# Where SBUF operands start modulo 512 bytes, and a third buffer for the stick-breaking weights, in a hybrid attention layer

## The chip, the core and the metric

The kernel runs on one core of a Trainium2 chip. A core has the matrix engine TensorE (PE; its weight loads are shown apart as PEld), VectorE (DVE), ScalarE (ACT), GpSimd (POOL) and SyncE (SP), which here only issues DMAs. The engines share the memory SBUF, 128 partitions wide; PE writes its results to PSUM, which has eight banks of 512 fp32 columns. Each engine takes its instructions in the order of its own program, and engines wait for each other by semaphores. The metric is the device time of one execution in microseconds (us), the median over the runs.

## The reference

One decoder layer on 1024 tokens of 1024 channels. The parts that matter here:

```python
u = rms_norm(h, norm1_g) * (1 + scale1) + shift1
z = u @ w_in                    # queries, keys, values, gates of both attentions, m_a, m_b
y_a = nsa_attention(...) @ w_up_nsa            # 8 heads of 64, sparse attention
y_b = stick_breaking_attention(q_b, k_b, v_b) @ w_up_sb      # 8 heads of 64
h = h + gate1 * ((sigmoid(m_a) * y_a + sigmoid(m_b) * y_b) @ w_out)
u2 = rms_norm(h, norm2_g) * (1 + scale2) + shift2
h = h + gate2 * (square(relu(u2 @ mlp_w1)) @ mlp_w2)         # 4096 hidden channels

def stick_breaking_attention(q, k, v):         # per block of 128 queries
    z = einsum('bqhd,bshd->bhqs', q, k) * 64 ** -0.5
    mask = key_pos < query_pos
    log_keep = where(mask, log_sigmoid(-z), 0)
    suffix = cumsum(log_keep, reverse) - log_keep
    a = where(mask, exp(log_sigmoid(z) + suffix), 0)
    return a @ v
```

So a weight is sigmoid(z) times the product of sigmoid(-z) over the keys between it and the query. All is in float32.

## The kernel before

Every large product is done in three: each operand is split into a high part, rounded to the matmul's fp32r type, and a low part, the rest (`hi` and `lo`, L63 and L66 among others), and PE adds high by high, high by low and low by high. A matmul has a stationary operand of 128 columns, loaded first, and a moving operand, mostly of 512 columns; a matmul below is named by its line. In its rows "px<-mth,wh" the first name behind the arrow is the moving operand, the second the stationary one.

The stages follow each other on PE, in us of the profiled span: loading and the first projections (0 to 120), keys and values of the sparse attention (L588, to 186), the sparse attention (214 to 604), the stick-breaking attention (623 to 857), the up projections of both attentions' outputs (L1324, 879 to 973), the output projection (L1428, to 1084) and the MLP (to the end). The rest of the input projection (L746) is cut into units and laid between the matmuls of the two attentions as filling; 96 of its matmuls run alone from 857 to 879.

In the up projection a unit is 12 matmuls of L1324 into one PSUM bank: four blocks of 128 channels, three products each, with the weights' parts wh and wl stationary and the attention output's parts oh and ol moving. Units of the two attentions (branch 0, sparse; branch 1, stick-breaking) alternate; oh and ol of the two branches lie in two pools, and wh and wl in one. In the MLP a hidden unit is 24 matmuls of L1512 with weights wh, wl stationary and the normalised input mth, mtl moving, 64 units in all. The second product of the MLP (L1561) is done by seven products of half-size blocks instead of eight, with the hidden activations' parts rah, ral stationary and the second weights' parts wbh, wbl moving.

Stick-breaking goes head by head, with three kinds of chunks: kind 0 is query rows 0 to 3 (of 128 queries each) with all their keys, 512, 384, 256 and 128 of them; kind 1 is rows 4 to 7 with their last 512 keys; kind 2 is rows 4 to 7 with their earlier keys, 512 down to 128. A chunk takes these steps:
- PE: scores into one of three PSUM banks psx (L1123 and L1124 with the key's two parts, L1126 adds the diagonal's mask).
- ACT: sigmoid of the scores into a tile sig (L1128), and sigmoid of their negatives in place in the bank (L1129). The tile is named sigr in kind 1 (five buffers), and after its width in kinds 0 and 2 (sig512, sig384, sig256, sig128; two buffers each).
- DVE: a running product over the bank, backwards, into a tile Pt (L1138). After it the bank can take another chunk.
- POOL: sig times Pt, in place (L1140).
- PE: the finished 128x128 pieces of sig are transposed into a bank pt (L1155); ACT and DVE split it into th and tl (L1163, L1164), and PE multiplies these with the values into the bank po (L1175).

The sig tile is free for another chunk when the last transposes out of it are done.

The kernel's code gives the work in a sequence; a scheduler then orders each engine's instructions, from its own estimates of their durations and from what has to wait for what, the reuse of buffers included. Tiles come from pools, stacked from the left or the right end of SBUF: a pool's offset follows from the sizes of those stacked before it on its side. A tile's place modulo 512 bytes in its partition therefore hangs on all tiles before it.

Of the kernel before, what the change touches and what calls it, by code (L numbers as in the profile page):

```python
# [6 lines left out]
F32 = mybir.dt.float32  # L7
# [10 lines left out]
NT = 8  # L18
# [17 lines left out]
def build(tc, I, out):  # L36
# [3 lines left out]
    def pool(name, side=None, bufs=1, **kw):  # L40
        if side:
            kw.update(side=side, reuse_waits="tile")
        p = tc.alloc_tile_pool(name=name, bufs=bufs, **kw)
        opened.append(p)
        return p
# [80 lines left out]
    pre_l = pre.tile([128, NK, 128], F32R, name="uwl")  # L126
    p1a = pool("p1a", "left")

    pool("odd", "right").tile([128, 8], F32, name="odd")
    xt_pool = pool("xt", "right")  # L130


# [263 lines left out]
    kvp = pool("kv", "right")  # L396
    kT = kvp.tile([128, 4, S], F32R, name="kT")
    vS = kvp.tile([128, NT, 4, 2, HD], F32R, name="vS")
    kcT = kvp.tile([128, 2, HD], F32R, name="kcT")
    gates = kvp.tile([128, NT, 8, 3], F32, name="gates")  # L400
    vC = kvp.tile([HD, 2, 2, HD], F32R, name="vC")
    bnp = pool("bn", "right")
    Bn = bnp.tile([128, 8, 256], F32, name="Bn")
# [177 lines left out]

    def kv_mm(t):
        raw = pb.tile([128, 544], F32, name="kvr", bufs=2)
        for c, (c0, c1) in enumerate(((0, 272), (272, 536))):
            p = (pd, psx)[c]()
            for k in range(NK):
                for n, (a, b) in enumerate(three(k, slice(t * 128, (t + 1) * 128))):
                    nc.tensor.matmul(p[:, :c1 - c0], a, ws[k][b][:, c0:c1],  # L588
                                     start=(k == 0 and n == 0), stop=(k == NK - 1 and n == 2))
            nc.scalar.copy(raw[:, c0:c1], p[:, :c1 - c0])  # L590
        return raw
# [59 lines left out]
    for n, (kind, t) in enumerate(jobs):  # L651
# [8 lines left out]
        if kind == "q":  # L660
            b = q_mm(t)
# [6 lines left out]
        else:  # L668
            if t == 0:
                ws = wk  # L670
            b = kv_mm(t)
# [86 lines left out]
    at = pool("at", "right")  # L758
# [43 lines left out]

    PT_ = 0.216


    def nsa_a(i, kv, hp, qT, P):
        n0, n1 = max(0, i - 1), i + 1
        x0 = 256 - (n1 - n0) * 128
        nb = 8 * i + 8
        chunks = plan(i)  # L810
        ngm = at.tile([128, 2, 2, 3], F32, name="ngm", bufs=2)
        sms = at.tile([128, 2, 2, 3], F32, name="sms", bufs=2)
        if len(chunks) < 6:
            nc.vector.memset(ngm, 3e38)
            nc.vector.memset(sms, 0.0)
# [1 line left out]
        for g in range(2):  # L817
            h = kv * 4 + hp * 2 + g
            q0, q1 = qT[0][:, hp * 2 + g], qT[1][:, hp * 2 + g]
            for br, c, a, b in chunks:  # L820
                n = (b - a) * 128
                p = psx()
# [26 lines left out]
        p = psx()  # L849
        for g in range(2):  # L850
            for q in range(2):
# [3 lines left out]
        sc = at.tile([128, 2, HD], F32, name="sc", bufs=2)  # L855
        nc.vector.tensor_tensor(sc[:, :, :nb], p[:, :128].rearrange("p (g c) -> p g c", g=2)[:, :, :nb],
                                Bc[:, kv * 4 + hp * 2:kv * 4 + hp * 2 + 2, 56 - 8 * i:56 - 8 * i + nb], op=OP.add)
        mc = at.tile([128, 2], F32, name="mc", bufs=2)
        nc.vector.tensor_reduce(mc, sc[:, :, :nb], axis=AX.X, op=OP.max, negate=True)
        nc.vector.scalar_tensor_tensor(sc[:, :, :nb], mc[:, :, None].to_broadcast([128, 2, nb]), 1e20, sc[:, :, :nb],  # L860
                                       op0=OP.min, op1=OP.add)
        pcx = at.tile([128, 2, HD], F32, name="pcx", bufs=2)
        P["c"] = pcx

        mm = at.tile([128, 2, 2], F32, name="mm", bufs=2)
        nc.vector.tensor_reduce(mm, ngm, axis=AX.X, op=OP.min)
        fc = at.tile([128, 2, 2, 3], F32, name="fc", bufs=2)
        nc.vector.tensor_tensor(fc, mm[:, :, :, None].to_broadcast([128, 2, 2, 3]), ngm, op=OP.subtract)
        yield 0.43
        nc.scalar.activation(pcx[:, :, :nb], sc[:, :, :nb], AF.Exp)  # L870
        nc.scalar.activation(fc, fc, AF.Exp)
        yield 0.0
        tot = at.tile([128, 3, 2], F32, name="tot", bufs=2)
        nc.vector.tensor_reduce(tot[:, 0], pcx[:, :, :nb], axis=AX.X, op=OP.add)
        nc.vector.tensor_tensor(sms, sms, fc, op=OP.mult)
        nc.vector.tensor_reduce(tot[:, 1:3], sms, axis=AX.X, op=OP.add)
# [10 lines left out]
    def nsa_b(i, kv, hp, P):  # L887
# [66 lines left out]
            yield cost  # L954
        tmp = at.tile([64, 256], F32, name="otmp", bufs=2)
        nc.scalar.copy(tmp, po_[64:128, :256])
        o = at.tile([64, 256], F32, name="osum", bufs=2)
        nc.vector.tensor_tensor(o, po_[0:64, :256], tmp, op=OP.add)
        h0 = (kv * 4 + hp * 2) * HD
        nc.sync.dma_start(oa_d[h0:h0 + 128, i * 128:(i + 1) * 128].rearrange("(g d) q -> d g q", g=2),  # L960
# [93 lines left out]


    def sb_gens(sp):
        zero = sp.tile([128, 16], F32, name="zero")[:, 0:1]
        nc.vector.memset(zero, 0.0)

        def load(u, h):  # L1060
# [54 lines left out]
        def sb_a(kind, chunk, ops, A, edges):  # L1115

            i, c0, c1 = chunk
            Q, Kh, Kl = ops
            w = c1 - c0
            p = psx()  # L1120
            qs = Q[:, i * 128:(i + 1) * 128]
            diag = kind != 2
            track(nc.tensor.matmul(p[:, :w], qs, Kh[:, c0:c1], start=True, stop=False))  # L1123
            track(nc.tensor.matmul(p[:, :w], qs, Kl[:, c0:c1], start=False, stop=not diag))  # L1124
            if diag:
                track(nc.tensor.matmul(p[:, w - 128:w], identr, diagr, start=False, stop=True))  # L1126
            sig = sp.tile([128, w], F32, name="sigr" if kind == 1 else "sig%d" % w, bufs=5 if kind == 1 else 2)
            nc.scalar.activation(sig, p[:, :w], AF.Sigmoid, scale=HD ** -0.5)  # L1128
            nc.scalar.activation(p[:, :w], p[:, :w], AF.Sigmoid, scale=-(HD ** -0.5))  # L1129
            A[i, kind] = (sig, c0)  # L1130

            def fin():
                Pt = sp.tile([128, 528], F32, name="Pt", bufs=6)
                if diag:
                    nc.vector.memset(Pt[:, w:w + 1], 1.0)
                else:
                    nc.vector.tensor_copy(Pt[:, w:w + 1], edges.pop(i)[:, 0:1])
                nc.vector.tensor_tensor_scan(Pt[:, 0:w][:, ::-1], p[:, 0:w][:, ::-1], zero.to_broadcast([128, w]),  # L1138
                                             1.0 if diag else Pt[:, w:w + 1], op0=OP.mult, op1=OP.add)
                nc.gpsimd.tensor_tensor(sig, sig, Pt[:, 1:w + 1], op=OP.mult)  # L1140
                if kind == 1:
                    edges[i] = Pt
            return fin, max(w, 256) * 2 / 2400.
# [469 lines left out]
```

## Time and profile before

| | us |
|---|---|
| median of three runs | 1754.13 (1746.5 to 1754.78) |
| the profiled execution, whole | 1753.26 |
| its span, first to last instruction | 1751.5 |
| PE busy, share of the span | 1694.7, 97% |
| DVE, POOL, ACT busy | 1141.8, 876.1, 819.8 |
| TensorE's mean granted clock | 0.989 |

The profile's busy times say which engine has work at all times; the table by stage says in which stretch PE has gaps. A matmul's duration in the rows reaches past the start of the next one, because matmuls are pipelined: what one costs in a row of them is the difference between starts. A wait stands in brackets behind the instruction that waited, with what released it.

### The profile page before, as it was taken

The numbers are of one execution on the slowest core, as the hardware profiler recorded it, in microseconds if no ns is written. First come the engines' busy times: TensorE is split into PE (matmuls) and PEld (weight loads), VectorE is DVE, ScalarE is ACT, GpSimd is POOL, SyncE is SP. The second block draws the span as 40 slices with busy tenths as digits, with TensorE's granted clock in tenths as the row PEclk, the third lists the DMA queues.
The fourth block names the chain that finished last, engine by engine and source line by source line (L and its number), as shares of the span: only waits on it lengthen the run. The fifth ranks groups of instructions, "written<-read, shape, count | busy, mean of one in ns | idle before, by whom it ended". The sixth has DMA issues, their size and how long they took to land.

```text
span 1751.5 us, 25194 instructions
## 1 busy us (share of the span) xinstructions
PE 1694.7 (97%) x8652; PEld 1414.9 (81%) x8652; DVE 1141.8 (65%) x2514; ACT 819.8 (47%) x1809; POOL 876.1 (50%) x824
## 2 busy tenths in 40 slices
PE   5999999999999989999999899999999999999998
PEld 4879888888888867788778688888888888888886
DVE  7597478778777567878464564365656575756458
ACT  6433476666666466766433244333333333333332
POOL 0021143434333387865164400786857675858676
PEclk8999999999999989999999999999999999999999
DMA  9365311111121264531485611121212020202102
GB/s 304 97 185 160 109 46 55 55 54 54 49 61 38 62 167 124 157 88 46 135 256 183 216 37 73 38 71 37 70 39 73 25 73 25 72 25 72 41 21 97
DMA packets 153656, 157.14 MB, mean 90 GB/s; under 512 B 13544, under 2 KB 117688, under 8 KB 153528
## 3 DMA queue, kind: packets, MB, share of 16 engines
q1 hardware_dynamic: 149304, 153.42, 29.3%
q10 hardware_dynamic: 4224, 2.10, 0.4%
q8 instruction: 69, 1.13, 0.3%
q14 instruction: 59, 0.48, 0.1%
HBM read 128.21 MB, written 27.28 MB: 89 GB/s over the span
## 4 chain that ended last, share of the span: by engine, by line
PE 83%; DMA 5%; DVE 4%; POOL 3%; ACT 3%; issue 2%; SPq 1%; POOLq 0%; DVEq 0%; ACTq 0%
PE px L1512 20%; PE px L1561 16%; PE pd L746 15%; PE px L1428 5%; PE po L909 4%; PE pt L943 4%; PE px L1324 3%; DMA adraw<-in_ada_w_dram 2%; PE psx L825 2%; PE psx L826 2%; PE cb L302 1%; PE pd L588 1%; PE po L1175 1%; PE psx L588 1%; PE pt L1155 1%
## 5 line engine op out<-in xcount | busy, mean ns | idle before, releaser
L1564 DVE TENSOR_TENSOR acc<-acc,px 128x512 f32<-128x512 f32 x384 | 243.9, 683 | 119.8 <-PE px L1561 114.5
L1512 PE MATMUL px<-mtl,wh 128*128 128x512 f32 x512 | 202.9, 396 | 0.0
L1512 PE MATMUL px<-mth,wl 128*128 128x512 f32 x512 | 202.7, 396 | 0.0
L1512 PE MATMUL px<-mth,wh 128*128 128x512 f32 x512 | 202.5, 396 | 0.0
L746 PE MATMUL pd<-uh,uwh 128*128 128x512 f32 x448 | 181.3, 405 | 0.7 <-ACT zo L1018 0.7
L1561 PE MATMUL px<-wbl,rah 128*128 128x512 f32 x448 | 175.3, 391 | 2.2 <-POOL wbl L1537 1.9
L746 PE MATMUL pd<-ul,uwh 128*128 128x512 f32 x448 | 177.1, 395 | 0.0
L746 PE MATMUL pd<-uh,uwl 128*128 128x512 f32 x448 | 177.1, 395 | 0.0
L1561 PE MATMUL px<-wbh,ral 128*128 128x512 f32 x448 | 174.9, 390 | 0.0
L66 DVE TENSOR_TENSOR wl<-raw,wh 128x1024 fp32r<-128x1024 f32 x48 | 76.3, 1591 | 149.1 <-ACT wh L61 128.7
L1561 PE MATMUL px<-wbh,rah 128*128 128x512 f32 x448 | 172.1, 389 | 0.0
L1537 POOL TENSOR_TENSOR wbl<-raw,wbh 128x1024 fp32r<-128x1024 f32 x40 | 106.0, 2649 | 91.9 <-ACT wbh L1536 91.6
L1523 POOL TENSOR_TENSOR w<-w,grow 128x1024 f32<-128x1024 f32 x32 | 82.8, 2602 | 97.0 <-DVE grow L1296 96.4
L901 DVE TENSOR_TENSOR tl<-pt,th 128x512 fp32r<-128x512 f32 (+8 forms) x168 | 103.7, 620 | 34.3 <-ACT th L900 33.0
L1535 POOL TENSOR_TENSOR raw<-r 128x512 f32<-128x512 f32 x80 | 109.9, 1397 | 20.0 <-DVE wl L66 17.9
L900 ACT CAST th<-pt 128x512 fp32r<-128x512 f32 (+8 forms) x168 | 88.8, 531 | 60.6 <-PE pt L943 58.0
L1512 PEld LDWEIGHTS px<-mth,wl 128*128 128x128 f32 x512 | 96.2, 188 | 23.6 <-issue 0.5
L1512 PEld LDWEIGHTS px<-mtl,wh 128*128 128x128 f32 x512 | 96.3, 188 | 23.0 <-issue 0.2
L1512 PEld LDWEIGHTS px<-mth,wh 128*128 128x128 f32 x512 | 96.2, 188 | 22.9 <-issue 0.2
L1536 ACT CAST rah<-raw 128x1024 fp32r<-128x1024 f32 x40 | 42.1, 1052 | 153.1 <-PE px L1561 139.7
L1561 PEld LDWEIGHTS px<-wbl,rah 128*128 128x128 f32 x448 | 84.1, 188 | 22.1 <-POOL wbl L1537 3.1
L746 PEld LDWEIGHTS pd<-uh,uwl 128*128 128x128 f32 x448 | 84.7, 189 | 18.1
(322 smaller groups left out, 4548.3 us busy)
## 6 DMA issues: line engine op xcount, KB each, us to landing
raw<-in_mlp_w_dram SPq DMA_DIRECT2D x32, 512.0 KB, 4.0
w<-in_mlp_w_dram SPq DMA_DIRECT2D x32, 512.0 KB, 4.0
z_d<-zo SPq DMA_DIRECT2D x56, 256.0 KB, 2.2
uwr<-in_w_in_dram SPq DMA_DIRECT2D x54, 256.0 KB, 3.0
adraw<-in_ada_w_dram SPq DMA_DIRECT2D x48, 256.0 KB, 2.9
xa<-in_ada_w_dram SPq DMA_DIRECT2D x32, 256.0 KB, 6.1
zr<-z_d SPq DMA_DIRECT2D x32, 256.0 KB, 4.8
m<-z_d SPq DMA_DIRECT2D x32, 256.0 KB, 3.6
```

The lines of the kernel that those rows point to most:

```text
L66: (nc.vector if e == "v" else nc.gpsimd).tensor_tensor(dst, src, f(h), op=OP.subtract)
L746: r = nc.tensor.matmul(p, a, b, start=(k == 0 and n == 0), stop=(k == NK - 1 and n == 2))
L900: nc.scalar.copy(th[:rows, :w], p[:rows, :w])
L901: nc.vector.tensor_tensor(tl[:rows, :w], p[:rows, :w], f(th)[:rows, :w], op=OP.subtract)
L909: track(nc.tensor.matmul(po_[:, :256], w, tt[q][:rows, m * 256:(m + 1) * 256], start=(n == 0 and m == 0 and q == 0), stop=(n == last and m ...
L1428: nc.tensor.matmul(p, a[:, k, ts_], b[:, k % 2], start=(k == 0 and n == 0), stop=(k == NK - 1 and n == 2))
L1512: nc.tensor.matmul(p, a[:, k], b[th][:, k], start=(k == 0 and m == 0), stop=(k == NK - 1 and m == 2))
L1523: nc.gpsimd.tensor_tensor(t, t, grow2, op=OP.mult)
L1535: nc.gpsimd.tensor_tensor(d, block(i0, j0, s), block(i1, j1, s), op=OP.add if sg > 0 else OP.subtract)
L1537: (nc.vector if e == "v" else nc.gpsimd).tensor_tensor(l.rearrange("p s n -> p (s n)"), src, f(h).rearrange("p s n -> p (s n)"), op=OP.sub ...
L1561: nc.tensor.matmul(p, a[:, s, qs], b[:, s], start=(s == 0 and n == 0), stop=(s == 1 and n == 2))
L1564: nc.vector.tensor_tensor(acc[:, t, ds_], acc[:, t, ds_], p, op=OP.add if sg > 0 else OP.subtract)
```

## The change

The tile "odd", which nothing uses and which stands first on the right side, grows from 8 to 88 columns, 32 to 352 bytes. All pools on the right move down by 320 bytes, so that what lay at 448 bytes modulo 512 lies at 128. The small tiles of the sparse attention get 64 columns each, osum 288, gates 256, Pt 640 and zero 128, which brings the tiles after them to 128 too. The key and value projection is cut at column 256 and no longer at 272. The tiles sig512, sig384, sig256 and sig128 get three buffers each for two; sigr keeps five.

Where the operands start, in bytes modulo 512, from the pools' layout (moving / stationary):

| matmul | before | after |
|---|---|---|
| L1512 (MLP, hidden units) | 128 / 448 | 128 / 128 |
| L1561 (MLP, second product) | 128 / 128 | 128 / 128 |
| L1324, branch 0 | 448 / 448 | 128 / 128 |
| L1324, branch 1 | 128 / 448 | 128 / 128 |
| L1428 (output projection) | 448 / 128 | 128 / 128 |
| L746 (filling) | 128 / 128 | 128 / 128 |
| sparse attention, scores | 192 / 384 | 128 / 128 |
| sparse attention, weights by values | 448 / 192 and 448 | 128 / 128 |
| L1123, L1124 (stick-breaking scores) | 64 / 64 | 128 / 128 |
| L1175 (weights by values) | 448 / 64 | 128 / 128 |
| sig tiles (for L1155) | 64 and 448 | 128 |

```diff
-    pool("odd", "right").tile([128, 8], F32, name="odd")
+    pool("odd", "right").tile([128, 88], F32, name="odd")
...
-    gates = kvp.tile([128, NT, 8, 3], F32, name="gates")
+    gates = kvp.tile([128, 256], F32, name="gates")[:, :NT * 24].rearrange("p (t h s) -> p t h s", t=NT, h=8)
...
-        for c, (c0, c1) in enumerate(((0, 272), (272, 536))):
+        for c, (c0, c1) in enumerate(((0, 256), (256, 536))):
...
+    def small(name, n=12):
+        return at.tile([128, 64], F32, name=name, bufs=2)[:, :n]
...
-        ngm = at.tile([128, 2, 2, 3], F32, name="ngm", bufs=2)
-        sms = at.tile([128, 2, 2, 3], F32, name="sms", bufs=2)
+        ngm, sms = (small(n).rearrange("p (b g c) -> p b g c", b=2, g=2) for n in ("ngm", "sms"))
...
-        o = at.tile([64, 256], F32, name="osum", bufs=2)
+        o = at.tile([64, 288], F32, name="osum", bufs=2)[:, :256]
...
-        zero = sp.tile([128, 16], F32, name="zero")[:, 0:1]
+        zero = sp.tile([128, 128], F32, name="zero")[:, 0:1]
...
-            sig = sp.tile([128, w], F32, name="sigr" if kind == 1 else "sig%d" % w, bufs=5 if kind == 1 else 2)
+            sig = sp.tile([128, w], F32, name="sigr" if kind == 1 else "sig%d" % w, bufs=5 if kind == 1 else 3)
...
-                Pt = sp.tile([128, 528], F32, name="Pt", bufs=6)
+                Pt = sp.tile([128, 640], F32, name="Pt", bufs=6)
```

(The tiles mc, mm, fc and tot become `small` in the same way as ngm and sms.) The lines of the changed kernel stand two further down from L805 on and three further from L959 on: L1128 becomes L1131, L1155 becomes L1158.

The scheduler orders the stick-breaking stage anew from the second head on; the other stages keep their order. Two places show how. The first is ACT at the third head's chunks of kind 0; sig_9120, sig_9155 and sig_9186 are their sig tiles of 512, 384 and 256 columns. Before:

```order
L1163 CAST th<-pt 128x256
L1163 CAST th<-pt 128x384
L1097 CAST V<-pt 128x4x64 x2
L441 ACTIVATE adraw<-adraw,cs 128x256
L1128 ACTIVATE sig_9186<-psx 128x256
L1129 ACTIVATE psx<-psx 128x256
L1128 ACTIVATE sig_9155<-psx 128x384
L1129 ACTIVATE psx<-psx 128x384
L1163 CAST th<-pt 128x512
L1128 ACTIVATE sig_9120<-psx 128x512
L1129 ACTIVATE psx<-psx 128x512
L1163 CAST th<-pt 128x128
```

And now:

```order
L1131 ACTIVATE sig_9120<-psx 128x512
L1132 ACTIVATE psx<-psx 128x512
L1166 CAST th<-pt 128x128
L441 ACTIVATE adraw<-adraw,cs 128x256
L1100 CAST V<-pt 128x4x64
L1182 COPY otmp<-po 64x512
L1100 CAST V<-pt 128x4x64
L1021 COPY zo<-pd 128x512
L1131 ACTIVATE sig_9155<-psx 128x384
L1132 ACTIVATE psx<-psx 128x384
L1131 ACTIVATE sig_9186<-psx 128x256
L1132 ACTIVATE psx<-psx 128x256
```

The three chunks now pass ACT in the order of their widths and ahead of the casts th of 256 and 384 columns that stood before them.

The second is PE at the last of the same chunks, that of 128 columns. The scores run ahead of the transposes by about a head: sig_8730, sig_8759, sig_8794 and sig_8824 are the kind 0 tiles of the head before, whose pieces are transposed there, and the chunks of 512 columns are the next ones, of kind 1. Before:

```order
L1175 MATMUL po<-th,V 128x384
L1155 MATMUL pt<-ident,sig_8824 128x128
L1155 MATMUL pt<-ident,sig_8794 128x128
L1155 MATMUL pt<-ident,sig_8759 128x128
L1155 MATMUL pt<-ident,sig_8730 128x128
L1175 MATMUL po<-tl,V 128x384
L1155 MATMUL pt<-ident,sigr 128x128
L1123 MATMUL psx<-Kh,Q 128x128
L1124 MATMUL psx<-Kl,Q 128x128
L1126 MATMUL psx<-diagr,identr 128x128
L1175 MATMUL po<-th,V 128x512
L1123 MATMUL psx<-Kh,Q 128x512
```

And now:

```order
L1126 MATMUL psx<-Kh,Q 128x128
L1127 MATMUL psx<-Kl,Q 128x128
L1129 MATMUL psx<-diagr,identr 128x128
L1158 MATMUL pt<-ident,sig_8759 128x128
L1158 MATMUL pt<-ident,sig_8730 128x128
L1178 MATMUL po<-th,V 128x128
L1178 MATMUL po<-tl,V 128x128
L1158 MATMUL pt<-ident,sig_8794 128x128
L1158 MATMUL pt<-ident,sig_8759 128x128
L1158 MATMUL pt<-ident,sig_8730 128x128
L1126 MATMUL psx<-Kh,Q 128x512
L1127 MATMUL psx<-Kl,Q 128x512
```

The chunk of 128 columns stood behind all ten transposes of those four tiles and now stands ahead of them, directly behind the chunks of 384 and 256 columns; two chunks of 512 columns follow, where filling stood.

## Rows read from the trace of the kernel before

**Rows 1.** Page, part 1: busy us, share of the span, instructions of each engine.

```profile
PE 1694.7 (97%) x8652; PEld 1414.9 (81%) x8652; DVE 1141.8 (65%) x2514; ACT 819.8 (47%) x1809; POOL 876.1 (50%) x824
```

**Rows 2.** By stage: start:end, length, busy PE PEld DVE ACT POOL, clock, DMA.

```profile
623.00:857.00 234.00, 216.92 (x1160) 179.31 (x1158) 176.65 (x339) 159.59 (x366) 155.58 (x162) 0.97 0.37 101
...
1084.00:1751.00 667.00, 661.59 (x2860) 536.51 (x2858) 396.92 (x490) 224.68 (x309) 470.09 (x264) 1.00 0.17 51
```

**Rows 3.** PE's waits from 1084 us on: us in total, times, longest.

```profile
PE px L1561 <- POOL wbl L1537: 1.9, 3, 1.3
```

**Rows 4.** Timeline of PE in the MLP: start, duration in us, engine, line, operation.

```profile
1401.52 0.39 PE L1561 MATMUL px<-wbh,rah 128*128 128x512 f32 x1
...
1403.59 0.39 PE L1561 MATMUL px<-wbh,rah 128*128 128x512 f32 x1
...
1406.99 0.40 PE L1512 MATMUL px<-mth,wh 128*128 128x512 f32 x1
...
1412.58 0.39 PE L1561 MATMUL px<-wbh,rah 128*128 128x512 f32 x1
```

**Rows 5.** Page, part 5, costliest groups: busy us, mean ns, idle before.

```profile
L1512 PE MATMUL px<-mtl,wh 128*128 128x512 f32 x512 | 202.9, 396 | 0.0
...
L746 PE MATMUL pd<-ul,uwh 128*128 128x512 f32 x448 | 177.1, 395 | 0.0
...
L1561 PE MATMUL px<-wbh,ral 128*128 128x512 f32 x448 | 174.9, 390 | 0.0
```

**Rows 6.** Timeline of PE in the up projection: first matmuls of three units.

```profile
953.78 0.39 PE L1324 MATMUL px<-oh,wh 128*128 128x512 f32 x1
...
956.52 0.39 PE L1324 MATMUL px<-oh,wh 128*128 128x512 f32 x1
...
959.32 0.39 PE L1324 MATMUL px<-oh,wh 128*128 128x512 f32 x1
```

**Rows 7.** Groups of PE by line and shape, 857 to 879 us.

```profile
L746 PE MATMUL pd<-ul,uwh 128*128 128x512 f32 x32 | 12.5, 389 | 0.0
```

**Rows 8.** Timeline of PE in the output projection, twelve matmuls apart.

```profile
1012.59 0.39 PE L1428 MATMUL px<-wh,mth 128*128 128x512 f32 x1
...
1015.34 0.39 PE L1428 MATMUL px<-wh,mth 128*128 128x512 f32 x1
```

**Rows 9.** Line L1128: how long ACT stood before it, until what.

```profile
  PE pt L1155: 16.0, 17
```

**Rows 10.** Timeline of all engines, 677.5 to 679.5 us; waits in brackets.

```profile
677.56 0.60 PE L1155 MATMUL pt<-ident,sig 128*128 128x128 f32 x4
...
677.98 0.39 ACT L1128 ACTIVATE sig<-psx 128x256 f32<-128x256 f32 x1 [0.57 <-PE pt L1155]
...
678.67 1.75 DVE L1138 TENSOR_TENSOR_SCAN Pt<-psx,zero 128x256 f32<-128x256 f32 x2 [2.51 <-ACT psx L1129]
...
679.42 0.33 PE L1123 MATMUL psx<-Kh,Q 128*128 128x128 f32 x1 [0.97 <-DVE Pt L1138]
```

**Rows 11.** PE's waits from 623 to 857 us, the first line.

```profile
PE psx L1123 <- DVE Pt L1138: 11.2, 7, 5.2
```

**Rows 12.** Timeline of PE at other waits of L1123.

```profile
632.09 0.48 PE L1123 MATMUL psx<-Kh,Q 128*128 128x128 f32 x1 [5.24 <-DVE Pt L1138]
...
701.75 0.44 PE L1123 MATMUL psx<-Kh,Q 128*128 128x384 f32 x1 [1.31 <-DVE Pt L1138]
...
734.83 0.27 PE L1155 MATMUL pt<-ident,sigr 128*128 128x128 f32 x1
...
736.06 0.33 PE L1123 MATMUL psx<-Kh,Q 128*128 128x128 f32 x1 [0.97 <-DVE Pt L1138]
...
792.70 0.33 PE L1123 MATMUL psx<-Kh,Q 128*128 128x128 f32 x1 [1.03 <-DVE Pt L1138]
```

**Rows 13.** Groups of ACT and DVE, 623 to 857 us: busy, mean ns.

```profile
L1129 ACT ACTIVATE psx<-psx 128x384 f32<-128x384 f32 x16 | 7.9, 494 | 0.0
...
L1138 DVE TENSOR_TENSOR_SCAN Pt<-psx,zero 128x384 f32<-128x384 f32 x8 | 7.6, 953 | 0.6
```

More of the change, by code (lines that the diff above doesn't have):

```diff
@@ L857, in nsa_a @@
                                 Bc[:, kv * 4 + hp * 2:kv * 4 + hp * 2 + 2, 56 - 8 * i:56 - 8 * i + nb], op=OP.add)
-        mc = at.tile([128, 2], F32, name="mc", bufs=2)
+        mc = small("mc", 2)
         nc.vector.tensor_reduce(mc, sc[:, :, :nb], axis=AX.X, op=OP.max, negate=True)
@@ L863, in nsa_a @@
         P["c"] = pcx
-        mm = at.tile([128, 2, 2], F32, name="mm", bufs=2)
+        mm = small("mm", 4).rearrange("p (b g) -> p b g", b=2)
         nc.vector.tensor_reduce(mm, ngm, axis=AX.X, op=OP.min)
-        fc = at.tile([128, 2, 2, 3], F32, name="fc", bufs=2)
+        fc = small("fc").rearrange("p (b g c) -> p b g c", b=2, g=2)
         nc.vector.tensor_tensor(fc, mm[:, :, :, None].to_broadcast([128, 2, 2, 3]), ngm, op=OP.subtract)
@@ L872, in nsa_a @@
         yield 0.0
-        tot = at.tile([128, 3, 2], F32, name="tot", bufs=2)
+        tot = small("tot", 6).rearrange("p (b g) -> p b g", b=3)
         nc.vector.tensor_reduce(tot[:, 0], pcx[:, :, :nb], axis=AX.X, op=OP.add)
```

## The prediction

> **What bounds the kernel now.** I read the engines' busy shares first. PE is busy for 97% of the span, the next engine, DVE, for 65% [rows 1]. So the time is PE's: its matmuls at their spacing, plus its gaps. The table by stage shows where either can move. From 1084 us on (the MLP) PE is busy for 661.6 of 667 us. From 623 to 857 us (stick-breaking attention, with the input projection's products L746 as filling) it is busy for 216.9 of 234 us, so some 17 us there are gaps [rows 2]. In the MLP the longest line of PE's waits is 1.9 us in all, for the tile wbl [rows 3]. The change touches two things: where matmul operands start, which can move the spacing, and the weights' buffers in stick-breaking, which can move gaps.
>
> **Offsets: the spacing in the trace.** The MLP has two kinds of product with the same shape, 128x512. Those of L1512 read operands at 128 (moving) and 448 (stationary) modulo 512, those of L1561 at 128 and 128. One stretch shows both. From 1406.99 to 1412.58 us there are 24 of L1512: 5.59 / 24 = 232.9 ns each. The 24 of L1561 before them take 1401.52 to 1406.99, 5.47 / 24 = 227.9 ns, and their last 15, from 1403.59 on, 3.40 / 15 = 226.7 ns [rows 4]. By the groups the mean durations say the same, 396 ns against 390 [rows 5]; ends overlap the next start, so the spacing counts and not the duration. A closer control is the up projection L1324: same line, same weights' place (448), and one branch's attention outputs at 448, the other's at 128. Units of 12 matmuls alternate between the branches: from 953.78 to 956.52 us 2.74 us for the branch at 448, from 956.52 to 959.32 us 2.80 us for that at 128 [rows 6]. So two operands at the same offset are spaced some 227.5 ns, two at different offsets some 233. That the offset is the cause is an inference: nothing else I see differs between the two branches.
>
> The terms, each on PE's own path, since PE hardly waits in these stages:
> - L1512: 512 x 3 = 1536 matmuls [rows 5] go from 128/448 to 128/128. At 227.9 ns they gain 1536 x 5.0 = 7.7 us, at 226.7 ns 9.5 us. I take 8.6. The lower bound comes from L746, which is at 128/128 already: the mean duration of one of its three products is 395 ns over all stages, with other engines busy [rows 5], and 389 in the stretch where it runs alone [rows 7], so traffic can hide part of the gain; half of 7.7, 3.9 us, stays as that bound.
> - L1324: 384 matmuls, half of them in the slow branch: 192 x 0.06 us / 12 = 1.0 us. Its other branch goes from 448/448 to 128/128, equal before and after: 0.
> - L1428 goes from 448/128 to 128/128. It runs 12 matmuls from 1012.59 to 1015.34 us, 229.2 ns each [rows 8], 384 in all: between 384 x 1.3 and 384 x 2.5 ns, 0.5 to 1.0. I take 0.7.
> - L1561 and L746 stay at 128/128: 0. The narrow matmuls of sparse attention and of stick-breaking change offsets too, but I see no difference between them that would price it: 0, with up to 2 us of gain kept for the range. The kv projection is split 256 + 280 for 272 + 264, the same 536 columns: 0. Padded tiles (the small sums, Pt, zero) add bytes and no instruction: 0.
>
> Sum of the offsets: 8.6 + 1.0 + 0.7 = **10.3 us less** (bounds 5 and 14). What comes next if PE is quicker in the MLP: POOL, busy for 470 of 667 us there, makes wbl, for which PE already waits 1.9 us in three places [rows 2, 3]. A gain of 9 us over 64 units, 0.14 us each, leaves POOL far from being the bound; up to 1 us could go there, within the bounds.
>
> The Trainium skill speaks against this term. "SBUF — State Buffer", section "SBUF: two separate sides", says that PE has ports of its own and never waits on anyone, so that where an operand lies should not matter; by that the term would be 0. The two branches of L1324 disagree with it here, 2.80 against 2.74 us.
>
> **Buffers: what goes.** In stick-breaking a score chunk passes PE (L1123, L1124, L1126), ACT (L1128 into a sig tile, L1129 in place in its PSUM bank), DVE's scan of that bank (L1138), POOL's product, and PE's transposes (L1155). Three psx banks hold chunks between PE and the scan. With two buffers a new sig waits for the transposes of the chunk two before in its width: ACT stood at L1128 16.0 us for L1155, in 17 places [rows 9]. PE pays where the banks fill. From 677.98 us ACT, released by L1155, makes the 256 and the 384 chunk one after the other; the scan stood 2.51 us; PE's next score came at 679.42, 0.97 us after PE could have gone on [rows 10]. PE's waits for the scan sum to 11.2 us in 7 places [rows 11]. The longest, 5.24 us at 632.09, is the start of the stage, before any buffer is reused. Of the others four are like that one or like each other, at 679.42, 701.75, 736.06 and 792.70 us (0.97, 1.31, 0.97 and 1.03) [rows 10, 12]: 4.3 us, and from the start of PE's instruction ahead, less its own 0.11 (734.83 to 736.06 us: 1.12), some 5.0. I let **5.0 us** go. The sig waits of ACT that PE does not feel are worth nothing.
>
> **Buffers: what comes.** Freed of that wait, the scheduler puts scores ahead of the transposes. In the second place shown with the change PE now does three chunks (384, 256, 128), five transposes and two small products, then two chunks of 512. The first of these needs the bank of the 384 chunk. PE's work between: the chunk itself, 384/512 x 2 x 0.23 + 0.06 = 0.41 us, the 256 chunk 0.30, the 128 chunk 0.18, five transposes at (0.60 - 0.27) / 3 = 0.11 us (four against one, [rows 10, 12]), 0.55, two products 0.12: 1.56 us. The bank comes free after 0.41 + 0.49 + 0.49 (both activations of 384 columns) + 0.95 (scan) [rows 13] = 2.34 us, with hand-overs some 2.5. So PE waits about 1 us there, and 0.3 us at the next chunk, which queues behind that scan. Eight places of the new order have less PE work between a bank's use and its reuse than its chain takes (1.6 to 2.8 us against 2.2 for 256, 2.5 for 384 and 3.2 for 512 columns); by the same sum they come to some 7 us. Below, it is 0: wherever PE arrives late for another reason, the bank is free. Above, it is 14 us, if each of them also meets one other step of about 0.6 to 0.7 us on ACT or DVE (a th cast, a tl difference). I take **6 us**, near the sum, since an earlier wait shortens a later one. Net of the buffers: 6.0 - 5.0 = 1 us more, from 5 less to 9 more. The 2nd to 4th sigr of a head still wait for transposes as before; these now stand farther ahead of them on PE.
>
> **Sum.** The profiled execution took 1753.3 us, its span 1751.5; it is 0.9 us below the median of the three runs, 1754.1. 1753.3 - 10.3 + 1.0 = **1744**. Its own range, from the bounds that are likely together, is 1739 to 1749.
>
> **The rivals.**
> - *No new waits.* The scores come earlier and ACT and DVE follow in step, so only the 5 us go, and other gaps of the 17 close a little: 1753.3 - 10.3 - 5.0 = 1738. For it: PE has gaps on pt and po too that earlier scores could fill. Against: the 1.56 us against 2.34 above.
> - *The banks cost twice that.* 14 us of new waits: 1753.3 - 10.3 + 9 = 1752. For it: DVE is busy for 177 and ACT for 160 of the 234 us [rows 2], so a chunk often meets other work. Against: the waits cannot add where PE is late already.
> - *Offsets do nothing*, and the difference of spacing belongs to the tiles' traffic: 1753.3 + 1 = 1754. For it: in the busy stages L746 is slow at 128/128. Against: the two branches of L1324. The rule of the Trainium skill's SBUF page above would give this, too.
> - *Slower.* Three chunks fill the banks with no filling queued before the next score, and ACT stands behind th casts whose transposes PE has not reached; then each head pays as much as the stage's start, 5.24 us [rows 12], in 7 heads: 36.7 - 5.0 - 10.3 = 21 us more, 1775. It decides from 19 + 5 = 24 us of new waits on (10.3 of gain and the 0.5% of 8.8 together), that is 3.4 us per head. For it: in order, PE cannot pass a score that waits. Against: the filling stands close behind in each place, and no wait but the first was over 1.4 us.
>
> **How the numbers follow.** The forecast has 0.46 (0.36 of it below 1745.4, the point 0.5% under the median, which is about what a measurement of this kernel can tell from no change; 0.10 above), no new waits 0.18, banks twice 0.17, offsets nothing 0.13, slower 0.06. Faster: 0.36 + 0.18 = 0.54; same: 0.10 + 0.17 + 0.13 = 0.40; slower 0.06. The range from 1734 to 1755 leaves out the slower case, the lower edge of the second and single runs beyond these ends, some 0.15.
>
> **What would show it.** L1512 spaced 227 to 228 ns, so that the MLP takes some 658 us for 667; L1324's branches equal; no wait of sig for the transposes; and PE's waits for the scan at the first 512 chunks behind a run of three. The prediction is wrong if L1512 stays at 233 ns, if the score waits stay under 8 us in all, or if they pass 20.

## The result and the profile after

The changed kernel takes 1741.56 us, the median of six runs (1736.53 to 1746.47), against 1754.65 us for the kernel before: 13 us less, a ratio of 0.9934 with a 95% interval of 0.9914 to 0.9953. The forecast was 1744. The profiled execution took 1741.55 us, 11.7 less than that of before.

The page of the changed kernel, its busy times and the costliest matmuls of the MLP, which answer to [rows 1] and [rows 5] (L1515 was L1512, L1564 was L1561):

```profile
PE 1678.6 (96%) x8652; PEld 1414.4 (81%) x8652; DVE 1147.0 (66%) x2514; ACT 818.2 (47%) x1809; POOL 871.9 (50%) x824
...
L1515 PE MATMUL px<-mtl,wh 128*128 128x512 f32 x512 | 199.6, 390 | 0.0
...
L1564 PE MATMUL px<-wbh,ral 128*128 128x512 f32 x448 | 174.3, 389 | 0.0
```

The two kinds of MLP product now last alike, 390 and 389 ns, for 396 and 390. The starts say it more exactly. The timeline of PE in the MLP after, the first matmuls of three runs of 24, for [rows 4]:

```profile
1389.82 0.39 PE L1515 MATMUL px<-mth,wh 128*128 128x512 f32 x1
...
1395.26 0.39 PE L1564 MATMUL px<-wbh,rah 128*128 128x512 f32 x1
...
1400.70 0.39 PE L1515 MATMUL px<-mth,wh 128*128 128x512 f32 x1
```

Both take 5.44 us, 226.7 ns each, where it was 5.59 and 5.47. The up projection, three units of 12, for [rows 6]:

```profile
951.35 0.39 PE L1327 MATMUL px<-oh,wh 128*128 128x512 f32 x1
...
954.07 0.39 PE L1327 MATMUL px<-oh,wh 128*128 128x512 f32 x1
...
956.79 0.39 PE L1327 MATMUL px<-oh,wh 128*128 128x512 f32 x1
```

The branches are equal now, 2.72 us each. Where the 11.7 us lie, by the first matmul of each stage in the two traces, in us:

| stretch | before | after | difference |
|---|---|---|---|
| start to the first score of stick-breaking | 623.45 | 621.88 | -1.6 |
| stick-breaking, first score to last product | 233.66 | 234.80 | +1.1 |
| filling alone | 22.11 | 22.12 | 0.0 |
| up projection | 95.36 | 94.27 | -1.1 |
| output projection, to the MLP's first matmul | 101.85 | 103.05 | +1.2 |
| MLP, first to last matmul | 670.95 | 659.55 | -11.4 |

The first line is no work of the change: kernels that share its code up to there begin stick-breaking between 621.7 and 624.0 us.

In stick-breaking ACT no longer waits for the transposes at the sig tiles of kinds 0 and 2. The line of the activation in the changed kernel, how long ACT stood before it and until what, for [rows 9]:

```profile
  PE psx L1129: 12.3, 12
  PE psx L1127: 8.1, 7
  PE pt L1158: 3.9, 6
```

The 3.9 us are the tiles sigr, which kept their five buffers. ACT now waits for PE's scores, and PE for the banks. PE's waits from 615 to 860 us, the first three lines, for [rows 11]:

```profile
PE psx L1126 <- DVE Pt L1141: 10.0, 10, 5.2
PE psx L1126 <- DVE Pt L1138: 5.8, 5, 2.8
PE pt L1158 <- DVE tl L1167: 1.6, 3, 0.9
```

At the scores it was 11.2 and 0.5 us, now it is 10.0, 5.8 and 0.7; all of PE's waits in this stage sum to 16.6 us before and 20.0 after. From 650 us on the score waits are 4.8 us in five places before and 9.7 us in fourteen after.

### The profile page after: what moved, and what is told of

It reads as the page before. It is cut to its first block, busy times and chain, and to the rows that moved or that the text cites. A ratio compares the mean times of both kernels' runs of the same rounds, so it can differ in the third digit from the quotient of the medians.

```text
span 1739.8 us, 25223 instructions
## 1 busy us (share of the span) xinstructions
PE 1678.6 (96%) x8652; PEld 1414.4 (81%) x8652; DVE 1147.0 (66%) x2514; ACT 818.2 (47%) x1809; POOL 871.9 (50%) x824
## 4 chain that ended last, share of the span: by engine, by line
PE 82%; DVE 5%; DMA 4%; POOL 3%; ACT 3%; issue 2%; SPq 1%; POOLq 0%; DVEq 0%; ACTq 0%
PE px L1515 20%; PE px L1564 16%; PE pd L746 15%; PE px L1431 5%; PE po L911 4%; PE px L1327 4%; PE pt L945 4%; DMA adraw<-in_ada_w_dram 2%; PE psx L827 2%; PE psx L828 2%; PE cb L302 1%; PE psx L588 1%; PE pd L588 1%; DVE Pt L1141 1%; PE pt L1158 1%
## 5 line engine op out<-in xcount | busy, mean ns | idle before, releaser
L1515 PE MATMUL px<-mtl,wh 128*128 128x512 f32 x512 | 199.6, 390 | 0.0
L1515 PE MATMUL px<-mth,wl 128*128 128x512 f32 x512 | 199.4, 390 | 0.0
L1515 PE MATMUL px<-mth,wh 128*128 128x512 f32 x512 | 199.2, 389 | 0.0
L746 PE MATMUL pd<-uh,uwh 128*128 128x512 f32 x448 | 180.9, 404 | 0.7 <-ACT zo L1021 0.7
L746 PE MATMUL pd<-ul,uwh 128*128 128x512 f32 x448 | 177.3, 396 | 0.0
L1564 PE MATMUL px<-wbl,rah 128*128 128x512 f32 x448 | 174.8, 390 | 2.1 <-POOL wbl L1540 1.8
L746 PE MATMUL pd<-uh,uwl 128*128 128x512 f32 x448 | 176.2, 393 | 0.0
L1564 PE MATMUL px<-wbh,ral 128*128 128x512 f32 x448 | 174.3, 389 | 0.0
L1564 PE MATMUL px<-wbh,rah 128*128 128x512 f32 x448 | 171.9, 389 | 0.0
L1515 PEld LDWEIGHTS px<-mth,wl 128*128 128x128 f32 x512 | 96.1, 188 | 20.4 <-issue 0.5
L1515 PEld LDWEIGHTS px<-mth,wh 128*128 128x128 f32 x512 | 96.1, 188 | 20.1 <-issue 0.2
L1515 PEld LDWEIGHTS px<-mtl,wh 128*128 128x128 f32 x512 | 96.1, 188 | 20.1 <-issue 0.2
L1564 PEld LDWEIGHTS px<-wbl,rah 128*128 128x128 f32 x448 | 84.1, 188 | 21.1 <-POOL wbl L1540 3.0
L746 PEld LDWEIGHTS pd<-uh,uwl 128*128 128x128 f32 x448 | 84.6, 189 | 17.8
```

The costliest lines, as they stand in the source:

```text
L746: r = nc.tensor.matmul(p, a, b, start=(k == 0 and n == 0), stop=(k == NK - 1 and n == 2))
L1515: nc.tensor.matmul(p, a[:, k], b[th][:, k], start=(k == 0 and m == 0), stop=(k == NK - 1 and m == 2))
L1564: nc.tensor.matmul(p, a[:, s, qs], b[:, s], start=(s == 0 and n == 0), stop=(s == 1 and n == 2))
```

## The experiments

**Which half of the change brings the time.** Theory: the spacing of matmuls does, and the third buffer costs a little. Rival: the buffers and the new order do, and offsets nothing. Three kernels take the change apart.

The changed kernel with two buffers again:

```diff
-            sig = sp.tile([128, w], F32, name="sigr" if kind == 1 else "sig%d" % w, bufs=5 if kind == 1 else 3)
+            sig = sp.tile([128, w], F32, name="sigr" if kind == 1 else "sig%d" % w, bufs=5 if kind == 1 else 2)
```

> The change with two buffers again for the sig tiles of 512, 384, 256 and 128 columns; every matmul operand stays at 128 bytes modulo 512. Theory (the gain is the spacing of matmuls whose two operands stood at different offsets, the buffers are worth nothing): L1515 spaced 227 ns, the MLP 655 us long, time 1739 to 1742 us, within 2 us of the changed kernel; ACT waits at sig for the transposes again, some 16 us. Rival (the buffers and the new order bring the gain, the offsets nothing): L1515 at 233 ns, 1753 us or more.

Measured: 1738.34 us, ratio to the kernel before 0.9911 (0.9896 to 0.9927). L1515 is at 226.7 ns, the MLP 659.5 us long, and ACT waits at sig as before, in the same count of places. The line of the activation in this kernel:

```profile
  PE pt L1158: 16.1, 17
```

So the whole gain is there without the third buffer, and the buffers win back nothing of the 16 us that ACT stands.

The kernel before with three buffers and nothing else:

```diff
-            sig = sp.tile([128, w], F32, name="sigr" if kind == 1 else "sig%d" % w, bufs=5 if kind == 1 else 2)
+            sig = sp.tile([128, w], F32, name="sigr" if kind == 1 else "sig%d" % w, bufs=5 if kind == 1 else 3)
```

> The kernel before with three buffers for the sig tiles and nothing else; the MLP's operands stay at 128 and 448. Theory: L1512 at 233.5 ns, MLP 667 us, time 1754 to 1757 us (PE waits for the psx banks grow by some 5 us and its other gaps in stick-breaking shrink by nearly as much). Rival (buffers bring the gain): 1743 us or less.

Measured: 1757.15 us for 1753.28, ratio 1.0016 (1.0001 to 1.0030): slower, by 0.2 to 5 us. L1512 stays at 233.3 ns. PE's waits from 615 to 860 us in this kernel:

```profile
PE psx L1123 <- DVE Pt L1138: 10.1, 10, 5.6
PE psx L1123 <- DVE Pt L1135: 5.4, 5, 2.8
PE pt L1155 <- DVE tl L1164: 1.5, 3, 0.9
```

These are the lines of the changed kernel, in count and size: the buffers alone make the new waits.

The kernel before with the shift of the right side and nothing else:

```diff
-    pool("odd", "right").tile([128, 8], F32, name="odd")
+    pool("odd", "right").tile([128, 88], F32, name="odd")
```

> The kernel before with the first tile of the right side at 88 columns for 8 and nothing else: MLP, up and output projection read both operands at 128, the sparse attention 384 and 64 (scores), 128 and 384 (values), stick-breaking 256 and 256, 128 and 256. Theory: the whole gain, 1741 to 1744 us, with L1512 at 227 ns; up to 1 us less of it if the 512 column products by values (128 and 256) are 5 ns slower each. Rival (the padded tiles of the two attentions matter too): less than 9 us gained.

Measured: 1739.58 us, ratio 0.9922 (0.9907 to 0.9936). One number of the change carries the gain. The padded tiles of the two attentions add at most about 1 us (1738.34 against 1739.58, intervals that overlap).

**What in the offsets matters.** Up to here "at different offsets" rests on 128 against 448. Three kernels lengthen the weight tiles, so that the MLP's buffers start at four places while the moving operand keeps its own:

```diff
-        wh, wl = ((pool_ or L["wr"]).tile([128, D], F32R, name=name, bufs=n) for name in ("wh", "wl"))
+        wh, wl = ((pool_ or L["wr"]).tile([128, D + 16], F32R, name=name, bufs=n)[:, :D] for name in ("wh", "wl"))
```

> The changed kernel with the tiles wh and wl of the pool wr 64 bytes longer each, so that the four buffers of the MLP's weights start at 384, 448, 0 and 64 modulo 512, against 128 of the moving operand. Theory (only equal offsets are fast): L1515 spaced 229 to 234 ns at all four, none at 227; the MLP 664 to 671 us for 660. Rival 1 (448 alone is slow, as the one place tried so far): three of four at 227, MLP 661 us. Rival 2 (the spacing grows with the distance between the two offsets): 64 fastest, 384 slowest.

The second sets the first tile of the right side back to 8 columns besides:

> As the run with longer weight tiles, but with the first tile of the right side at 8 columns, so that the MLP's four weight buffers start at 192, 256, 320 and 384, the moving operand at 128. Theory (only equal offsets are fast): all four at 229 to 234 ns, MLP 664 to 671 us. Rival 1 (448 alone is slow): all four at 227, MLP 660 us. Rival 2 (distance): 192 fastest, 384 slowest.

The third puts `mt.tile([128, 48], F32, name="mtpad")` in front of mth and mtl instead:

> As the run with the weights at 384, 448, 0 and 64, with 192 bytes in front of the moving operands mth and mtl, which then start at 320; the second MLP product has both operands at 320. Theory (equal offsets are fast, wherever they are): L1565 at 320 and 320 spaced 227 ns, L1516 slower at all four. Rival 1 (128 is the good place): L1565 slower than 227 ns too. Rival 2 (distance): 384 the fastest, 0 or 64 the slowest.

A unit has 16 matmuls with a tile wh and 8 with a tile wl; two units in a row read the same buffer, the next two the other. The timeline of PE in the first of the three, one unit with wh at 384 and wl at 0, then one with wh at 448 and wl at 64; the unit ends where L1564 begins:

```profile
1396.45 0.39 PE L1515 MATMUL px<-mth,wh 128*128 128x512 f32 x1
...
1401.99 0.39 PE L1564 MATMUL px<-wbh,rah 128*128 128x512 f32 x1
...
1418.42 0.40 PE L1515 MATMUL px<-mth,wh 128*128 128x512 f32 x1
...
1423.98 0.39 PE L1564 MATMUL px<-wbh,rah 128*128 128x512 f32 x1
```

The second, a unit with 192 and 320, then one with 256 and 384:

```profile
1395.09 0.40 PE L1515 MATMUL px<-mth,wh 128*128 128x512 f32 x1
...
1400.65 0.39 PE L1564 MATMUL px<-wbh,rah 128*128 128x512 f32 x1
...
1417.15 0.40 PE L1515 MATMUL px<-mth,wh 128*128 128x512 f32 x1
...
1422.76 0.39 PE L1564 MATMUL px<-wbh,rah 128*128 128x512 f32 x1
```

The third, a unit with 384 and 0 against 320:

```profile
1391.23 0.40 PE L1516 MATMUL px<-mth,wh 128*128 128x512 f32 x1
...
1396.80 0.39 PE L1565 MATMUL px<-wbh,rah 128*128 128x512 f32 x1
```

The three kernels were run once each: 1752.43, 1752.87 and 1749.58 us, the MLP 667.2, 670.2 and 670.2 us long. All units are slower than 5.44 us, but not alike: 5.54, 5.56, 5.56, 5.61 and 5.57 us. The spacing sorts them. Taken for the matmuls by wh that are followed by another by the same wh (254 or 255 in each row, one spacing of over 300 ns left out), with the weights' start less the moving operand's:

| weights, moving | difference | modulo 256 | mean spacing, ns |
|---|---|---|---|
| 384, 128 | 256 | 0 | 226.8 |
| 448, 128 | 320 | 64 | 231.8 |
| 192, 128 | 64 | 64 | 231.9 |
| 384, 320 | 64 | 64 | 231.9 |
| 256, 128 | 128 | 128 | 233.1 |
| 448, 320 | 128 | 128 | 233.2 |

The rows fall into groups by the difference modulo 256, whatever the two starts are. That 448 alone is slow falls (192 and 256 are slow too), that the distance as such counts falls (64 is slow, 256 is fast), and so does what I had put as the theory, that only equal offsets are fast: 384 against 128 is as fast as 128 against 128. The second MLP product, at 320 and 320 in the third kernel, is spaced 227.3 ns, so 128 is no special place either. All these rows stand in chains in which wh and wl have different starts. Where the two take turns the spacing is 229 to 235 ns, in no order that the runs explain, so the whole units differ less than the rows. The one chain with a single difference other than 0 is that of the kernel before, 233.3 ns at 64 (448 against 128). That 64 costs less than 128, as the table has it, is therefore not shown; that both cost more than 0 is.

The theory in its new form was put to a kernel in which the offsets are unequal modulo 512 and 256 apart:

```diff
-    pool("odd", "right").tile([128, 8], F32, name="odd")
+    pool("odd", "right").tile([128, 24], F32, name="odd")
```

> The kernel before with the first tile of the right side at 24 columns for 8 and nothing else, so that what lay at 448 modulo 512 lies at 384: the MLP's moving operand at 128, its weights at 384, 256 bytes apart. Theory, formed from the runs with four weight offsets (the spacing follows the difference of the two starts modulo 256 bytes, and is least at zero): L1512 at 226.8 ns, L1324 at 227 in both branches, MLP 660 us, the whole gain, 1738 to 1742 us, though the offsets are unequal modulo 512. Rival (equal modulo 512 is needed): L1512 at 231 to 234 ns, 1750 to 1755 us.

Measured: 1739.01 us, ratio 0.9919 (0.9907 to 0.9931), the whole gain. The timeline of PE in this kernel's MLP, hidden units with weights at 384 against 128, between them the second product at 128 and 128:

```profile
1389.91 0.39 PE L1512 MATMUL px<-mth,wh 128*128 128x512 f32 x1
...
1395.36 0.39 PE L1561 MATMUL px<-wbh,rah 128*128 128x512 f32 x1
...
1400.80 0.39 PE L1512 MATMUL px<-mth,wh 128*128 128x512 f32 x1
```

5.45 and 5.44 us: no difference between 256 and 0 apart. Both branches of L1324 are at 227 ns there too (128 and 384 against 384).

A finer step was tried as well, with weight tiles 32 bytes longer:

```diff
+        wh, wl = ((pool_ or L["wr"]).tile([128, D + 8], F32R, name=name, bufs=n)[:, :D] for name in ("wh", "wl"))
...
+    pool("odd", "right").tile([128, 64], F32, name="odd")
```

> As the run with longer weight tiles, but 32 bytes longer each and with 64 columns in the first tile of the right side: the MLP's four weight buffers start at 96, 128, 160 and 192, the moving operand at 128, side by side in one run. Theory (only equal offsets are fast): the buffer at 128 at 227 ns, the other three at 229 to 234. Rival 1 (448 alone is slow): all four at 227. Rival 2 (distance): 96 and 160 alike and near 227, 192 slower.

Measured, counted as in the table: 228.6 ns at 128 (wl beside it at 192), 232.2 at 96 (wl at 160), 5.54 us for units of either kind, 1754.63 us in the one run. So 32 bytes apart are enough to lose the gain (232.2 ns), and the fast pair in a chain with a slow one does not quite reach 226.7. 96 is not near 227, so rival 2 falls here as well.

**What the third buffer's waits are.** In the changed kernel the profile names the memset of Pt (L1138) as what PE's scores waited for, 5.8 us. If that memset waited for a Pt tile that POOL still reads, a seventh tile would take the wait away:

```diff
-                Pt = sp.tile([128, 640], F32, name="Pt", bufs=6)
+                Pt = sp.tile([128, 528], F32, name="Pt", bufs=7)
...
-        zero = sp.tile([128, 128], F32, name="zero")[:, 0:1]
+        zero = sp.tile([128, 272], F32, name="zero")[:, 0:1]
```

> The changed kernel with seven Pt tiles of 528 columns for six of 640 (zero gets 272 columns for 128; the keys, queries and values of stick-breaking move to 192). In the changed kernel PE waits 5.8 us at the scores where the profile names the memset of Pt. Theory (that memset waits for the oldest of six Pt tiles, which POOL still reads, and the scan stands behind it): these 5.8 us go, 1737 to 1739 us. Rival (DVE and POOL are late anyway, the wait goes to the scan): PE's waits at the scores stay at 14 to 17 us, time 1740 to 1743 us.

Measured: 1743.24 us, ratio 0.9936 (0.9921 to 0.9952), no gain. PE's waits in this kernel:

```profile
PE psx L1126 <- DVE Pt L1141: 9.4, 10, 5.3
PE psx L1126 <- DVE Pt L1138: 5.8, 6, 2.8
```

The wait is unchanged, so the theory falls. The timeline of the changed kernel around its longest new wait shows what stands there; PE, ACT and DVE, 694 to 701 us:

```profile
694.85 0.39 PE L1126 MATMUL psx<-Kh,Q 128*128 128x512 f32 x1
...
696.35 1.03 ACT L1078 CAST Q<-zr 128x1024 fp32r<-128x1024 f32 x1
...
697.70 0.57 ACT L1131 ACTIVATE sig<-psx 128x512 f32<-128x512 f32 x1
...
698.79 1.22 DVE L1141 TENSOR_TENSOR_SCAN Pt<-psx,zero 128x512 f32<-128x512 f32 x1 [0.38 <-ACT psx L1132]
...
699.96 0.06 DVE L1138 MEMSET Pt<- 128x1 f32 x1
...
700.07 0.47 PE L1126 MATMUL psx<-Kh,Q 128*128 128x128 f32 x1 [2.81 <-DVE Pt L1138]
```

PE sends chunks of 512, 384 and 256 columns within 2.4 us, with only three transposes between them, and then stands until the first one's bank is free. ACT comes to that chunk only at 697.70, behind a cast of the next queries of 1.03 us and two steps of 0.5 us for another stage; the scan follows, and the memset named is only the instruction behind it, for the next chunk. What the wait hangs on is the scan of the bank three chunks back, by way of ACT's queue.

**Two buffers beside three, once more**, both kernels on one chip:

> The changed kernel once more, on the same chip as the next run. Theory (the third buffer costs 3 to 4 us of waits at the scores): 3 us slower than the changed kernel with two buffers, 1741 to 1743 us. Rival (no difference): within 1 us of it.

> The changed kernel with two buffers for the sig tiles, as before, beside the changed kernel on the same chip. Theory: 1738 to 1739 us, 3 us faster than the changed kernel. Rival: no difference.

Measured: 1739.11 us (mean 1741.1) for three buffers, 1737.73 us (mean 1738.4) for two, ratios to the kernel before 0.9931 (0.9916 to 0.9946) and 0.9915 (0.9902 to 0.9928). The intervals of this pair overlap. With the earlier runs the means are 1741.4 us over 12 runs and 1738.3 over 9, and PE's waits from 615 to 860 us sum to 20.0 and 18.2 us with three buffers, 15.3 and 16.4 with two. I take 3 us for the price of the third buffer, in line with the kernel that has it alone; this pair by itself does not show it. The profiled executions speak for nearly as much once those with the same granted clock are set side by side. In two of them the clock fell at 640 to 660 and at 700 to 740 us (0.91 and 0.96): there the stage took 234.8 us with three buffers and 232.2 with two. In two it was 1.00 in both stretches: 230.6 and 228.3 us. That is 2.6 and 2.3 us for the buffer. The changed kernel with two buffers has the lowest time of the versions here, though one padding tile alone (1739.58 and 1739.01 us) cannot be told from it.

**The stage's first wait.** It is the longest one in all of these kernels, 4.7 to 5.6 us. Filling was laid into it, in the changed kernel with two buffers:

```diff
+    BUMP = 9.0
...
                         late.append(fin)
                         yield cost
+                        if k == 0 and c == 2:
+                            yield BUMP
...
-    drive(sb_gens(sp), fill, 0.55, 0.08, TAIL)
+    drive(sb_gens(sp), fill, 0.52, 0.075, TAIL)
```

> The changed kernel with two buffers, and 23 matmuls of filling (5.2 us) between the third and the fourth score chunk of the first head, where PE stands 5.1 us; the filling behind it is given out 5% more slowly, so that the 96 matmuls behind the stage stay. Theory (that wait is the largest of the stage and hides under filling): 4 to 5 us less, 1734 us, and no 5 us wait at the scores. Rival (the filling is missing later, new gaps of the same size): 1738 to 1739 us.

Measured: 1740.49 us, ratio 0.9926 (0.9914 to 0.9938), no gain over two buffers alone. PE's longest waits in this kernel, in total, at the scores and at po:

```profile
PE psx L1127 <- DVE Pt L1142: 8.9, 12, 1.4
PE po L1179 <- ACT th L1167: 2.9, 3, 2.1
```

The long wait is gone and others have grown: none is over 2.1 us, and together they are some 15 us as before. Filling is a fixed sum, and what is spent at the start is missing later (this is argued from the unchanged sum, not shown). The rival was right.

## Why the prediction came out as it did

- **The step on which most rested was right**: in the MLP and the two projections ahead of it, matmuls of 512 columns whose operands start at the same offset are spaced 227 ns, and the change makes them so. The control that told it ahead was the two branches of L1324 in [rows 6]. The rival "offsets do nothing" fell. The Trainium skill ("SBUF — State Buffer", section "SBUF: two separate sides") says that PE never waits on anyone, where it speaks of engines that contend for ports. The step that the prediction built on it, that the place of PE's own two operands could then not matter, does not hold here: 6.6 ns per matmul hang on it. What inside the chip makes the difference, no run shows.
- **Its size was too small.** L1512 gained 233.3 - 226.7 = 6.6 ns, 1536 x 6.6 = 10.1 us, where I took 8.6 between 7.7 and 9.5. L1561, which I put at 0, gained too: 227.8 to 226.8 ns, 1344 x 1.0 = 1.3 us. I had seen that L1561 was slower in its first matmuls behind L1512 (227.9 over 24, 226.7 over the last 15, [rows 4]). For L1512 I then took the middle between the two as the pace to come, and for L1561 I took no gain. But the slow start was an after-effect of L1512 and went with it, so the steady 226.7 was the right pace for both lines. The pace before came from one unit, too, 232.9 ns, where it is 233.3 over all of them. Together the MLP gained 11.4 us for 8.6.
- **The up and the output projection** were to gain 1.0 and 0.7 us; together they gained nothing (197.2 us before, 197.3 after). The spacing did fall as forecast: in the slow branch of L1324 by 6 ns, in L1428 from 229.1 to 227.3 ns, 384 x 1.8 = 0.7 us. But PE has one wait in the output projection for a weight tile from POOL, and it grew. The line of it before and after:

```profile
PE px L1428 <- POOL wh L63: 4.9, 1, 4.9
...
PE px L1431 <- POOL wh L63: 6.4, 1, 6.4
```

  Counted from the first matmul of the up projection, PE comes to this tile at 100.5 us before and at 99.4 after, and the tile lets it go on at 105.4 and 105.8. I had not followed that wait: a PE that is quicker ahead of it comes earlier to a tile that does not come earlier. What PE saved ahead of the tile it stood longer for it, and of the 1.7 us nothing is left in these two traces. That the up projection by itself came out 1.1 us shorter, near the 1.0 forecast, decides nothing: in another execution of the changed kernel it took 96.4 us, longer than before.
- **The buffers** were forecast at 5.0 us gone and 6 us new, 1 us more. In the profiled executions the stage is 1.1 us longer, which fits by luck, since another execution of the same kernel took 4 us less; by the experiments the price is some 3 us. The steps were right in kind: ACT's wait for the transposes went, of the four waits of PE behind it three went and one shrank to 0.54 us, and others came where chunks stand close together. At the place that was worked out (1.56 us of PE's work against a chain of 2.5) PE waited 0.50 us for the 1.0 and 0.3 forecast, in the trace of the changed kernel at 672.67 us:

```profile
672.67 0.50 PE L1126 MATMUL psx<-Kh,Q 128*128 128x512 f32 x1 [0.50 <-DVE Pt L1138]
```

  The largest, 2.81 us, was at a place where the chain alone would not have stood so long: there ACT had other steps queued, as in the rival "the banks cost twice that". So the term that was sized wrongly is the new waits: 6 us were forecast, from a sum of 7 over eight places that had each chunk meet an idle ACT, and from 650 us on PE stands 9.7 us in fourteen. 4.4 us of them are at the last chunk of a head and the first of the next. At the scores the waits grew by 4.8 us net, on pt and po they shrank by 1.4; the rest, 3.4, agrees with the price of some 3 us.
- **The slower rival** did not come: no head paid what the start pays, the largest new wait was 2.81 us. Nor did "no new waits".
- In sum: the MLP gained 2.8 us more than forecast, the output projection came out 1.9 us worse, and 1.6 us at the start are no part of the change; 1744 - 2.8 + 1.9 - 1.6 is the 1741.5 of the profiled execution, within the range. The mechanism that carries the sum was right; that the total came within 2.5 us is in part luck, as its errors nearly cancel.

## What to carry to other kernels

Where PE is the bound, compare the start-to-start spacing of matmuls of one shape between lines; a few ns over thousands of matmuls were worth more here than the waits that the buffers moved, and a code line that runs with two layouts is the control that tells the layout from the rest. In this kernel weights and moving operand should start a multiple of 256 bytes apart, and one padding tile at the head of a side is enough. A buffer that frees a waiting engine is worth only what the bound engine feels of the wait, and it lets the scheduler bring work forward into the next scarce thing, here the PSUM banks: take it away again if the time does not show it.

## What the runs showed of the hardware that was not expected

- The spacing of the MLP's 128x512 fp32r matmuls hangs on the difference of the two operands' starts modulo 256 bytes: 226.8 ns at 0, 231.8 to 231.9 at 64, 233.1 to 233.2 at 128 in the chains of the table, the same to 0.1 ns at different absolute places, and 233.3 where all matmuls of a chain are at 64. The price is not the same everywhere: L1428, at 192 modulo 256 (448 moving, 128 stationary), was at 229.1 ns. And equal places do not ensure 227 ns: L577, a product of the first projections whose moving operand starts at 0, 128, 256 and 384 against 128, is spaced 231 to 233 ns at all four, before and after, and the filling L746 between the attentions' matmuls about 230 at 128 and 128; what sets these, no run shows. For 256 columns no such difference was seen: the sparse attention's scores with the queries' low part, 152 matmuls, have a median spacing of 118 ns where the starts differ by 192 modulo 256 (before) and 120 ns where they do not (after).
- The slow spacing reaches into the next product: 24 matmuls of a line with a good layout were at 227.8 ns behind a line with a bad one, and at 226.8 behind a good one.
- The granted clock of the stick-breaking stage falls behind PE's waits. The table by stretch in the changed kernel, where PE stands for 5.2 us up to 630.5 us (the third number from the end is the clock); read microsecond by microsecond it is 0.50, the lower of the two levels (1.2 GHz), from 629 to 635 us and 1.00 around that:

```profile
623.00:640.00 17.00, 11.80 (x53) 9.69 (x52) 9.84 (x19) 13.93 (x32) 15.43 (x17) 0.80 0.67 183
```

  and in the kernel with filling in that place:

```profile
623.00:640.00 17.00, 13.74 (x66) 10.62 (x64) 6.59 (x13) 9.99 (x24) 14.26 (x14) 1.00 0.85 229
640.00:660.00 20.00, 17.66 (x94) 14.86 (x95) 18.09 (x35) 17.48 (x42) 17.07 (x16) 0.91 0.40 106
```

  There the fall is only put off: PE stands 2.1 us up to 640.1 and 0.7 us up to 641.1, and the clock is at 0.50 from 641 to 644 us. Later dips (0.91 at 640 to 660 us, 0.96 at 700 to 740) come in some executions of a kernel and not in others: the stage was 228.3 and 232.2 us long in two executions of the kernel with two buffers, 234.8 and 230.6 in two of the changed one. A single profile of this stage therefore tells waits, and the times of several runs tell what they cost.
